# Mixture-of-experts stage: another order of the experts' steps, a 32-slot form for the smallest expert, seven weight tiles

## The chip, the cores and the metric

The kernel runs on one core of one Trainium2 chip, as one program. The metric is the device time in microseconds (us) of one execution. Lower is better.

## The reference, cut to what matters

Two transformer blocks run one after the other on 256 tokens of width 1024, in fp32. The change lies in the mixture of experts (MoE) at the end of the first block:

```
def _moe(h, router, w1, w3, w2):
    ...
    top_v, top_i = lax.top_k(logits, TOP_K)            # 2 of 8 experts per token
    top_w = jax.nn.softmax(top_v, axis=-1)
    gates = ...                                        # [256, 8], two entries per token
    for e in range(N_EXPERTS):
        y = y + gates[:, e:e + 1] * _swiglu(hf, w1[e], w3[e], w2[e])
```

`_swiglu` is silu(x w1) * (x w3), times w2, with w1 and w3 of 1024 x 3584 and w2 of 3584 x 1024. One expert's weights are 44 MB in fp32, eight are 352 MB. Which expert a token goes to is known only at run time.

## The kernel before, in words

Each expert's tokens are gathered into a fixed number of slots by a product with a 0/1 matrix, pass through the expert, and are scattered back by a second product (`scatter`), which adds gate * result to `k.y`. After the routing the experts are ranked by how many tokens they got. Expert "0" is always expert number FIRST, and 1 to 7 follow by falling count. Below, E0 to E7 are these ranks. `base_of` (line 220) gives the slots: 160 for E1, 64 for E5, E6 and E7 (`SMALL`), 128 for the others. If an expert got more tokens than slots, a branch after the stage (line 1351) handles the rest.

An expert's weights come as 42 units of 1 MB (28 of w1 and w3, 14 of w2). `k.unit` (line 239) takes the next of a ring of `MOE_RING` = 6 raw tiles and issues its DMA on SP's queue, in program order. A tile is free again when the work that reads it is done.

There are three ways of multiplying:

- **128 slots** (`expert`). `k.split` (lines 254, 255) splits half a unit into a high part `wh` (copied on ScalarE, "ACT") and a low part `wl` (subtracted on VectorE, "DVE"). Both come from the pool `k.whl`, with four buffers each. `mm3` (lines 266 to 268) makes three fp32r products of 512 columns on TensorE ("PE") out of each of the four 512-column pieces of a unit: 12 products a unit.
- **64 slots** (`small_expert`). Plain fp32 products straight from the raw tile, with the token block as the stationary operand of 64 columns, in two column groups of the array (lines 1192 and 1206). No split is needed.
- **E1's slots 128 to 159** (`extra`). The same in four column groups of 32 (lines 1090 and 1114), inside E1's loop. The raw tile is thus read by the split and by these products. The trace shows each plain fp32 product as two matmul instructions.

`expert` and `small_expert` are generators. One step of an expert (`run(todo[r], 1)`) is a block of 512 hidden units: four units of w1 and w3, silu and multiplication, then two units of w2 for the block before, then the transposition of the new hidden block. An expert has seven steps and an end (`run(todo[r])`) with the last two units of w2. The first step has no w2, so it has four units. `late` holds a finished expert's scatter until another expert calls `settle()`.

Order before: four steps of E0; preparation of E1; a step of E0; preparation of E5 to E7 (`smalls`); the rest of E0; then seven pairs of steps E1, E5; seven pairs E2, E6; E3 alone; E4 with E7, where E7 begins two steps later. E7 therefore has two steps and its end left when E4 is through. In between `y` is multiplied by a gate row and added to `Xx` (lines 1323 and 1324), and E4's and E7's scatters: E7 adds straight to `Xx` (mode "last"). Then the final norms are computed and the branch is taken.

The program is put in order by a scheduler at build time. It keeps each engine's instructions roughly, but not strictly, in the order in which the source issues them.

PSUM in this stage: `pA` has three banks (products, transpositions), `pO` two, `pX` three (the accumulators `po`). E0 accumulates in `pO`, E1 to E4 in `pX`, E5 to E7 in `pO`.

Of the kernel before, what the change touches and what calls it, by code (L numbers as in the profile page):

```python
# [213 lines left out]
MOE_RING = 6  # L214
CAP1 = 160
SMALL = (5, 6, 7)
LAST = 7


def base_of(r):  # L220

    return CAP1 if r == 1 else 64 if r in SMALL else 128

# [682 lines left out]
def moe(k):  # L906
# [147 lines left out]

    def expert(r, e, xe, ST, mode="add", extra=None):
# [12 lines left out]
        pool, name = (k.pO, "psO") if r == 0 else (k.pX, "psX")  # L1068
        po = [pool.tile([128, 512], F32, name=name) for _ in range(2 if extra is None else 3)]
        hid = None  # L1070
        for b in range(8):
            if b < 7:
                pss = []
                if extra is not None:
                    px = k.pA.tile([128, 512], F32, name="psA")
                for z in range(2):
                    ps = k.pA.tile([128, 512], F32, name="psA")
                    for h in range(2):
                        raw = k.unit(src(b * 4 + z * 2 + h))
                        for q in range(2):  # L1080
                            w = k.split(raw[:, q * 1024:(q + 1) * 1024], 1024)
                            for kk in range(2):
                                kc = h * 4 + q * 2 + kk
                                sl = slice(kk * 512, (kk + 1) * 512)
                                k.mm3(ps, (xH[:, kc, :], xL[:, kc, :]), (w[0][:, sl], w[1][:, sl]), kc == 0, kc == 7)
                        if extra is not None:
                            for kc in range(4 * h, 4 * h + 4):
                                for j in range(4):
                                    o = (kc % 4) * 512 + j * 128
                                    nc.tensor.matmul(px[32 * j:32 * j + 32, z * 128:(z + 1) * 128], xex[:, kc, :],  # L1090
                                                     raw[:, o:o + 128], start=(kc == 0), stop=(kc == 7))
                    pss.append(ps)
                s = k.tmp.tile([128, 512], F32, name="act", bufs=k.nact)
                nc.scalar.activation(s, pss[0], AF.Silu)
                m = k.tmp.tile([128, 512], F32, name="act2", tag="act", bufs=k.nact)
                nc.vector.tensor_mul(m, s, pss[1])
                if extra is not None:
                    sx = k.tmp.tile([128, 512], F32, name="actx", tag="act", bufs=k.nact)
                    nc.scalar.activation(sx[:, :128], px[:, 0:128], AF.Silu)
                    nc.vector.tensor_mul(sx[:, 128:256], sx[:, :128], px[:, 128:256])  # L1100
            settle()
            if b > 0:
                for u in (2 * b - 2, 2 * b - 1):
                    raw = k.unit(src(28 + u))
                    for q in range(2):
                        c = u * 2 + q
                        w = k.split(raw[:, q * 1024:(q + 1) * 1024], 1024)
                        cs = slice((c % 4) * 128, (c % 4) * 128 + 128)
                        for d in range(2):
                            sl = slice(d * 512, (d + 1) * 512)  # L1110
                            k.mm3(po[d], (hid[0][:, cs], hid[1][:, cs]), (w[0][:, sl], w[1][:, sl]), c == 0, c == 27)
                        if extra is not None:
                            for j in range(4):
                                nc.tensor.matmul(po[2][32 * j:32 * j + 32, 0:256], hid[2][:, 32 * (c % 4):32 * (c % 4) + 32],
                                                 raw[:, q * 1024 + j * 256:q * 1024 + (j + 1) * 256],
                                                 start=(c == 0), stop=(c == 27))
            if b < 7:
                pt = k.pA.tile([128, 512], F32, name="psA")
                for q in range(4):
                    nc.tensor.transpose(pt[:, q * 128:(q + 1) * 128], m[:, q * 128:(q + 1) * 128], k.ident)  # L1120
                hH = p.tile([128, 512], F32R, name=tag + "H", bufs=2)
                hL = p.tile([128, 512], F32R, name=tag + "L", bufs=2)
                nc.scalar.copy(hH, pt)
                nc.vector.tensor_sub(hL, pt, hH.bitcast(F32))
                hid = [hH, hL]
                if extra is not None:
                    pt = k.pA.tile([128, 512], F32, name="psA")
                    nc.tensor.transpose(pt[:, :128], sx[:, 128:256], k.ident)
                    hx = p.tile([128, 128], F32, name="hxx", bufs=2)
                    nc.vector.tensor_copy(hx, pt[:, :128])  # L1130
                    hid.append(hx)
                yield True
# [11 lines left out]
        if extra is not None:  # L1144
            oxs = []
            for d in range(2):
                ox = k.tmp.tile([128, 512], F32, name="ox", tag="act", bufs=k.nact)
                nc.gpsimd.memset(ox, 0.0)
                for j in range(2 * d, 2 * d + 2):
                    js = slice(32 * j, 32 * j + 32)  # L1150
                    nc.scalar.copy(ox[js, (j % 2) * 256:(j % 2) * 256 + 256], po[2][js, 0:256])
                oxs.append(ox)
# [20 lines left out]
    def small_expert(r, e, xf, i, Sd, mode="add"):  # L1173
# [41 lines left out]
        o = po  # L1215
        if mode == "last":
            o = k.tmp.tile([128, 512], F32, name="og", tag="act", bufs=k.nact)
            for t in range(2):
                ts_ = slice(64 * t, 64 * t + 64)
                nc.vector.tensor_mul(o[ts_, :], po[ts_, :], k.gate5[ts_, t * 512:(t + 1) * 512])  # L1220
        oH = p.tile([128, 512], F32R, name="oH", tag="hidH", bufs=2)
        oL = p.tile([128, 512], F32R, name="oL", tag="hidL", bufs=2)
        nc.scalar.copy(oH, o)
        nc.vector.tensor_sub(oL, o, oH.bitcast(F32))

        def scatter():
            for d in range(2):
                for t in range(2):
# [6 lines left out]
                    y = k.Xx if mode == "last" else k.y  # L1235
                    nc.vector.scalar_tensor_tensor(y[:, t, sl], ps, g, y[:, t, sl], op0=ALU.mult, op1=ALU.add)
# [17 lines left out]
    def smalls():  # L1254
# [5 lines left out]
        xf = gather(S, 64 * len(SMALL), "xs")  # L1260
        out = []
        for i in range(len(SMALL)):
# [7 lines left out]
            Z = p.tile([128, 512], F32R, name="Sz", tag="Sz" if SMALL[i] == LAST else "hxH",  # L1270
                       bufs=1 if SMALL[i] == LAST else 2)
# [5 lines left out]
        return out  # L1277
# [10 lines left out]
    Sx = p.tile([128, 2, 4, 32], F32R, name="Sx")  # L1288
    for t in range(2):
        nc.vector.tensor_copy(Sx[:, t], S[:, t, 128:160].bitcast(F32).unsqueeze(1).to_broadcast([128, 4, 32]))  # L1290
    SxT = slots_T(Sx.rearrange("p t j s -> p t (j s)"), "SxT")
    STx = slots_T(S[:, :, 0:128], "ST1")
    todo = {1: expert(1, index(1), xe, STx, "add", (xex, SxT.bitcast(F32)))}
    run(g, 1)
    for r, made in zip(SMALL, smalls()):
        todo[r] = small_expert(r, index(r), *made, "last" if r == LAST else "add")
    run(g)
    pairs = {}

    def start(r):  # L1300
        if r in (2, 3, 4):
            if r not in pairs:
                pairs.update(zip((r, r + 1), pair(r)))
            xf, z, ST = pairs[r]
            todo[r] = expert(r, index(r), parts(xf, z), ST)

    for one, other in ((1, 5), (2, 6), (3, None), (4, 7)):
        start(one)
        for b in range(7):
            run(todo[one], 1)  # L1310
            if other is not None and (other != LAST or b > 1):
                run(todo[other], 1)
        if one == 3:
# [3 lines left out]
        run(todo[one])  # L1317
        if other not in (None, LAST):
            run(todo[other])
    over = nc.values_load(infoi[0:1, 16:17], engines=ALL_ENGINES, min_val=0, max_val=256)  # L1320
    run(todo[LAST], 1)
    for t in range(2):
        nc.vector.tensor_mul(k.y[:, t, :], k.y[:, t, :], k.gate5)
        nc.vector.tensor_add(k.Xx[:, t, :], k.Xx[:, t, :], k.y[:, t, :])
    run(todo[LAST], 1)
    g = todo[LAST]
# [24 lines left out]
    with k.tc.If(over > 0):  # L1351
        for r in (0, 1, 2, 3) + SMALL:
# [553 lines left out]
def build(nc, tc, a, o):  # L1906
    with ExitStack() as es0:
# [6 lines left out]
        k.whl = k.pool("whl", 4)  # L1914
# [14 lines left out]
        with ExitStack() as es1:  # L1929
            k.es = es1  # L1930
            k.pA = k.pool("pA", 4, space=PSUM)
# [19 lines left out]
        with ExitStack() as es1:  # L1951
# [6 lines left out]
            k.pX = k.pool("pX2", 3, space=PSUM)  # L1958
            extra = k.pool("wraw2", MOE_RING - 5)
# [3 lines left out]
        with ExitStack() as es1:  # L1963
            k.es = es1
            k.nxn, k.nact = 2, 5
            k.tmp = k.pool("tmp4", 2)
            k.h2 = k.pool("h2")
# [23 lines left out]
```

## Time and profile before

| what | value |
|---|---|
| median of 3 runs | 2272.66 us (2270.87 to 2274.89) |
| the profiled execution | 2272.78 us |
| its span, first to last instruction | 2269.8 us |
| outside the span | 3.0 us |
| TensorE's mean granted clock | 0.983 of 2.4 GHz |
| PE / DVE / ACT busy | 2167.8 / 1413.6 / 1007.1 us |
| read from HBM | 546.08 MB |

The profiled execution is 0.1 us above the median, so it stands for it. The MoE's products run from about 797 to 1785 us of the span. PE's busy time counts overlapping instructions once, so inside the stage the starts of instructions say more than their durations.

### The profile page before, as it was taken

What the parts mean: (1) busy time and instruction counts of PE and PEld (TensorE: products, weight loads), DVE (VectorE), ACT (ScalarE), POOL (GpSimd) and SP (SyncE); (2) the same over time, 40 slices, a digit from 0 to 9 for tenths busy, and PEclk for the clock granted to TensorE, in tenths of its full rate; (3) what the DMA queues carried; (4) which work ended last, traced back from release to release, by engine and by line L of the source; (5) the groups of instructions that cost most, each with busy time, mean ns of one, the idle gap of its engine ahead of it and who ended that gap; (6) DMA issues with size and microseconds to landing.
All of it is one profiled execution on the core that took longest, in us unless ns stands there. A gap on an engine that the chain in (4) does not pass through costs nothing. (4 is left out here: it accounts for less than half of the span.)

```text
span 2269.8 us, 31775 instructions
## 1 busy us (share of the span) xinstructions
PE 2167.8 (96%) x12353; PEld 1639.3 (72%) x12353; DVE 1413.6 (62%) x2391; ACT 1007.1 (44%) x1452; POOL 51.0 (2%) x101
## 2 busy tenths in 40 slices
PE   6999999999999899999999999999999699999998
PEld 3777778788786777766656666677765477798997
DVE  4899339534555687743436454888555487866555
ACT  4234322222345477543335444677443344454443
POOL 1000000000000000000000000000000000000000
PEclk7999999999999999999999999999999899999999
DMA  9553545431543286788888999898999643344552
GB/s 369 213 201 120 210 149 195 162 140 49 170 170 112 99 310 263 289 338 342 330 347 316 413 421 421 342 361 312 348 421 421 267 154 117 107 165 166 186 186 75
DMA packets 82112, 554.55 MB, mean 244 GB/s; under 512 B 9905, under 2 KB 10161, under 8 KB 19233
## 3 DMA queue, kind: packets, MB, share of 16 engines
q1 hardware_dynamic: 75600, 531.87, 61.3%
q0 software_dynamic: 6208, 19.52, 2.5%
q8 instruction: 99, 1.62, 0.3%
q10 hardware_dynamic: 144, 1.05, 0.1%
q14 instruction: 61, 0.49, 0.1%
HBM read 546.08 MB, written 6.32 MB: 243 GB/s over the span
## 5 line engine op out<-in xcount | busy, mean ns | idle before, releaser
L255 DVE TENSOR_TENSOR wl<-raw,wh 128x1024 fp32r<-128x1024 f32 x664 | 791.5, 1215 | 379.3 <-ACT wh L254 372.8
L254 ACT CAST wh<-raw 128x1024 fp32r<-128x1024 f32 x664 | 679.3, 1045 | 651.6 <-PE psA L267 176.0
L266 PE MATMUL psA<-wh,xeH 128*128 128x512 f32 x560 | 228.3, 408 | 2.7 <-ACT wh L254 1.2
L267 PE MATMUL psA<-wl,xeH 128*128 128x512 f32 x560 | 226.3, 404 | 4.4 <-DVE wl L255 4.4
L268 PE MATMUL psA<-wh,xeL 128*128 128x512 f32 x560 | 223.1, 398 | 0.1
L266 PE MATMUL psG<-hH,wh 128*128 128x256 f32 x544 | 157.8, 290 | 1.0 <-DVE hL L699 1.0
L266 PE MATMUL psA<-xTH,wh 128*128 128x512 f32 x400 | 157.3, 393 | 0.0
L268 PE MATMUL psG<-hH,wl 128*128 128x256 f32 x544 | 155.8, 286 | 0.0
L267 PE MATMUL psA<-xTL,wh 128*128 128x512 f32 x400 | 155.7, 389 | 0.0
L268 PE MATMUL psA<-xTH,wl 128*128 128x512 f32 x400 | 155.7, 389 | 0.0
L267 PE MATMUL psG<-hL,wh 128*128 128x256 f32 x544 | 155.1, 285 | 0.0
L1192 PE MATMUL psA<-raw,xs 128*64 128x256 f32 x1344 | 150.3, 381 | 0.8 <-DMA raw<-in_moe_dram 0.4
L266 PEld LDWEIGHTS psA<-wh,xeH 128*128 128x128 f32 x560 | 106.3, 190 | 41.1 <-ACT wh L254 11.3
L1192 PEld LDWEIGHTS psA<-raw,xs 128*64 128x64 f32 x1344 | 94.5, 137 | 53.0 <-issue 5.3
L267 PEld LDWEIGHTS psA<-wl,xeH 128*128 128x128 f32 x560 | 106.5, 190 | 35.9 <-DVE wl L255 12.2
L268 PEld LDWEIGHTS psA<-wh,xeL 128*128 128x128 f32 x560 | 106.3, 190 | 25.0 <-DVE xeL L1046 0.9
L266 PEld LDWEIGHTS psG<-hH,wh 128*128 128x128 f32 x544 | 103.9, 191 | 13.3 <-issue 11.2
L268 PEld LDWEIGHTS psG<-hH,wl 128*128 128x128 f32 x544 | 103.9, 191 | 6.3 <-issue 6.2
L267 PEld LDWEIGHTS psG<-hL,wh 128*128 128x128 f32 x544 | 104.0, 191 | 3.3 <-issue 2.7
L1196 DVE TENSOR_TENSOR act<-act,psA 128x256 f32<-128x256 f32 x21 | 8.8, 421 | 141.2 <-ACT act L1195 141.2
L266 PEld LDWEIGHTS psA<-xTH,wh 128*128 128x128 f32 x400 | 75.1, 188 | 25.4 <-ACT wh L254 8.4
L267 PE MATMUL psX<-wl,hidH 128*128 128x512 f32 x224 | 89.9, 401 | 0.0
(576 smaller groups left out, 3776.8 us busy)
## 6 DMA issues: line engine op xcount, KB each, us to landing
raw<-in_moe_dram SPq DMA_DIRECT2D x336, 1024.0 KB, 7.4
raw<-in_w_ada_dram SPq DMA_DIRECT2D x48, 1024.0 KB, 6.4
raw<-in_w2ff_dram SPq DMA_DIRECT2D x32, 1024.0 KB, 4.8
raw<-in_w2mix_dram SPq DMA_DIRECT2D x24, 1024.0 KB, 4.8
raw<-in_eff_dram SPq DMA_DIRECT2D x22, 1024.0 KB, 4.9
raw<-in_eff_dram SPq DMA_DIRECT2D x22, 512.0 KB, 3.3
raw<-in_ein_dram SPq DMA_DIRECT2D x8, 1024.0 KB, 7.0
raw<-in_w2in_dram SPq DMA_DIRECT2D x8, 1024.0 KB, 9.3
```

The costliest lines, as they stand in the source:

```text
L254: self.nc.scalar.copy(h[:, :n], src)
L255: self.nc.vector.tensor_sub(l[:, :n], src, h[:, :n].bitcast(F32))
L266: mm(ps, s[0], m[0], start=first, stop=False)
L267: mm(ps, s[0], m[1], start=False, stop=False)
L268: mm(ps, s[1], m[0], start=False, stop=last)
L1192: nc.tensor.matmul(px[64 * t:64 * t + 64, z * 256:(z + 1) * 256], xf[:, kc, xs], raw[:, o:o + 256], start=(kc == 0), stop=(kc == 7))
L1196: nc.vector.tensor_mul(m[:, 256:512], m[:, 0:256], px[:, 256:512])
```

## The change

It gives the experts' steps another order, written out by hand (`ORDER`: a number is one step, a negative number -n the end of expert n-1). E7 gets 32 slots and its own generator, `tiny_expert`, which uses products like those of `extra`. These products are grouped: for E1, both halves of w1 or w3 behind each other after the 24 fp32r products (before: after each half), and a whole unit of w2 at once. The ring has seven raw tiles; for that `k.whl` has three buffers in this stage in place of four. E0 accumulates in `pX`. E4's scatter now goes to `Xx` too. E1's and the small experts' preparations come one behind the other, after four steps of E0. `gate5` and the load of `over` are issued at E3's first step, the fold of `y` into `Xx` after E4's first step.

```diff
-MOE_RING = 6
+MOE_RING = 7
-SMALL = (5, 6, 7)
-LAST = 7
+ORDER = ([0, 5, 0, 5, 0, 5, -1] + [1, 6, 5] * 4 + [-6] + [1, 6, 7, 1, 6, 7, 1, 6, -2, -7]
+         + [2, 2, 2, 2, 7, 2, 2, 2, -3] + [3, 7, 3, 3, 3, 3, 7, 3, 3, -4] + [4, 4, 7, 4, 4, 4, 4, 7, 4, -5])
+SMALL = (5, 6)
+TINY = 7
...
+    return CAP1 if r == 1 else 64 if r in SMALL else 32 if r == TINY else 128
...
+    def tiny_in(px, x, raw, z, h):
+        for kc in range(4 * h, 4 * h + 4):
+            for j in range(4):
+                o = (kc % 4) * 512 + j * 128
+                nc.tensor.matmul(px[32 * j:32 * j + 32, z * 128:(z + 1) * 128], x[:, kc, :],
+                                 raw[:, o:o + 128], start=(kc == 0), stop=(kc == 7))
...
+    def tiny_out(po, hx, raw, u):
+        for q in range(2):
+            c = u * 2 + q
+            for j in range(4):
+                nc.tensor.matmul(po[32 * j:32 * j + 32, 0:256], hx[:, 32 * (c % 4):32 * (c % 4) + 32],
+                                 raw[:, q * 1024 + j * 256:q * 1024 + (j + 1) * 256], start=(c == 0), stop=(c == 27))
...
+    def tiny_expert(r, e, x, SxT):
...
+        for b in range(8):
+            if b < 7:
+                px = k.pA.tile([128, 512], F32, name="psA")
+                for z in range(2):
+                    for h in range(2):
+                        tiny_in(px, x, k.unit(src(b * 4 + z * 2 + h)), z, h)
+                sx = tiny_gate(px)
+                settle()
+            if b > 0:
+                for u in (2 * b - 2, 2 * b - 1):
+                    tiny_out(po, hx, k.unit(src(28 + u)), u)
+            if b < 7:
+                hx = tiny_hid(sx)
+                yield True
...
+                    nc.tensor.matmul(ps, SxT[:, t * 128:(t + 1) * 128], oxs[d], start=True, stop=True)
...
-        pool, name = (k.pO, "psO") if r == 0 else (k.pX, "psX")
-        po = [pool.tile([128, 512], F32, name=name) for _ in range(2 if extra is None else 3)]
+        po = [k.pX.tile([128, 512], F32, name="psX") for _ in range(2 if extra is None else 3)]
...
-                        if extra is not None:
-                            for kc in range(4 * h, 4 * h + 4):
...
+                    if extra is not None:
+                        for h in range(2):
+                            tiny_in(px, xex, raws[h], z, h)
...
+                    if extra is not None:
+                        tiny_out(po[2], hid[2], raw, u)
...
-    run(g, 1)
-    for r, made in zip(SMALL, smalls()):
-        todo[r] = small_expert(r, index(r), *made, "last" if r == LAST else "add")
-    run(g)
+    made, (x7, S7) = smalls()
...
+    for r in ORDER:
+        if r < 0:
+            run(todo[-r - 1])
+            continue
+        if r not in todo:
+            start(r)
+        run(todo[r], 1)
...
-        k.whl = k.pool("whl", 4)
...
+            k.whl = k.pool("whl2", 3)
```

## Rows read from the trace of the kernel before

**Rows 1.** The page: engines' busy time; DMA issues (KB each, us to landing).
```profile
PE 2167.8 (96%) x12353; PEld 1639.3 (72%) x12353; DVE 1413.6 (62%) x2391; ACT 1007.1 (44%) x1452; POOL 51.0 (2%) x101
...
raw<-in_moe_dram SPq DMA_DIRECT2D x336, 1024.0 KB, 7.4
```

**Rows 2.** Windows: us; busy per engine (instructions); PE clock, DMA share, GB/s.
```profile
797.00:945.00 148.00, 141.36 (x679) 113.04 (x682) 123.44 (x145) 112.67 (x135) 0.00 (x0) 0.99 0.76 290
945.00:1200.00 255.00, 253.73 (x2179) 159.09 (x2172) 110.99 (x119) 94.91 (x119) 1.05 (x2) 1.00 0.87 335
1260.00:1400.00 140.00, 135.12 (x720) 92.38 (x718) 77.97 (x74) 68.07 (x78) 0.00 (x0) 1.00 1.01 421
1440.00:1600.00 160.00, 156.36 (x694) 123.20 (x693) 138.05 (x133) 117.03 (x134) 0.00 (x0) 1.00 0.88 334
1660.00:1760.00 100.00, 97.14 (x562) 63.58 (x563) 51.89 (x53) 37.77 (x47) 0.00 (x0) 1.00 1.01 420
```

**Rows 3.** Timeline of PE: 128-slot experts' transpositions, E0 alone, then E4 with E7.
```profile
845.02 0.60 PE L1120 MATMUL psA<-identt,act 128*128 128x128 f32 x4
...
862.25 0.60 PE L1120 MATMUL psA<-identt,act 128*128 128x128 f32 x4
...
1693.57 0.60 PE L1120 MATMUL psA<-identt,act 128*128 128x128 f32 x4
...
1723.14 0.60 PE L1120 MATMUL psA<-identt,act 128*128 128x128 f32 x4
```

**Rows 4.** Timeline of PE: one step of a 64-slot expert (start us, us).
```profile
1369.74 7.13 PE L1192 MATMUL psA<-raw,xs 128*64 128x256 f32 x64
1377.81 0.44 PE L1210 MATMUL psA<-identt,act 128*128 128x128 f32 x2 [0.94 <-DVE act L1196]
1378.18 3.65 PE L1206 MATMUL psO<-raw,hids 128*64 128x512 f32 x16
```

**Rows 5.** Groups by line, 783 to 1810 us: busy us, mean ns, idle before.
```profile
L1090 PEld LDWEIGHTS psA<-raw,xex 128*32 128x32 f32 x896 | 23.8, 109 | 12.1 <-issue 11.5 <-ACT wh L254 0.4 <-PE psA L1210 0.2
...
L1162 PE MATMUL psA<-ox,SxT 128*128 128x512 f32 x8 | 4.1, 591 | 0.0
...
L1323 DVE TENSOR_TENSOR y<-y,gate 128x1024 f32<-128x1024 f32 x2 | 2.3, 1214 | 0.0
```

**Rows 6.** Timeline of PE: blocks of 32-slot products inside E1's steps.
```profile
1154.67 0.62 PE L1090 MATMUL psA<-raw,xex 128*32 128x128 f32 x10
...
1161.43 0.39 PE L268 MATMUL psA<-wh,xeL 128*128 128x512 f32 x1
1161.75 1.08 PE L1090 MATMUL psA<-raw,xex 128*32 128x128 f32 x32
1162.77 0.50 PE L266 MATMUL psA<-wh,xeH 128*128 128x512 f32 x1
1163.10 0.40 PE L267 MATMUL psA<-wl,xeH 128*128 128x512 f32 x1
...
1187.12 1.07 PE L1114 MATMUL psX<-raw,hxx 128*32 128x256 f32 x16
```

**Rows 7.** Timeline of PE: the stage's last waits.
```profile
1774.62 5.25 PE L1206 MATMUL psO<-raw,hids 128*64 128x512 f32 x16 [3.12 <-DMA raw<-in_moe_dram]
1782.06 0.97 PE L1232 MATMUL psA<-oH,Sz 128*128 128x512 f32 x3 [2.19 <-ACT oH L1223]
```

**Rows 8.** Timeline of DVE, ACT and PE: one pair `wh`, `wl` in E0.
```profile
836.54 2.60 DVE L255 TENSOR_TENSOR wl<-raw,wh 128x1024 fp32r<-128x1024 f32 x2 [0.21 <-ACT wh L254]
...
836.82 1.06 ACT L254 CAST wh<-raw 128x1024 fp32r<-128x1024 f32 x1 [0.32 <-PE psA L268]
...
838.22 1.06 ACT L254 CAST wh<-raw 128x1024 fp32r<-128x1024 f32 x1 [0.34 <-PE psA L268]
...
840.46 0.68 DVE L1096 TENSOR_TENSOR act<-act,psA 128x512 f32<-128x512 f32 x1
...
841.05 0.40 PE L267 MATMUL psO<-wl,hidH 128*128 128x512 f32 x1
```

More of the change, by code (lines that the diff above doesn't have):

```diff
@@ new lines, in tiny_rows @@
+    def tiny_rows(po, gate=False):
+        oxs = []
+        for d in range(2):
+            ox = k.tmp.tile([128, 512], F32, name="ox", tag="act", bufs=k.nact)
+            nc.gpsimd.memset(ox, 0.0)
+            for j in range(2 * d, 2 * d + 2):
+                js = slice(32 * j, 32 * j + 32)
+                to = ox[js, (j % 2) * 256:(j % 2) * 256 + 256]
+                if gate:
+                    nc.vector.tensor_mul(to, po[js, 0:256], k.gate5[js, j * 256:(j + 1) * 256])
+                else:
+                    nc.scalar.copy(to, po[js, 0:256])
+            oxs.append(ox)
+        return oxs
@@ L1144, in expert @@
         if extra is not None:
[L1145 to L1152, printed above, removed]
+            oxs = tiny_rows(po[2])
         def scatter():
@@ L1214, in small_expert @@
         settle()
[L1215 to L1220, printed above, removed]
         oH = p.tile([128, 512], F32R, name="oH", tag="hidH", bufs=2)
         oL = p.tile([128, 512], F32R, name="oL", tag="hidL", bufs=2)
-        nc.scalar.copy(oH, o)
-        nc.vector.tensor_sub(oL, o, oH.bitcast(F32))
+        nc.scalar.copy(oH, po)
+        nc.vector.tensor_sub(oL, po, oH.bitcast(F32))
         def scatter():
@@ L1276, in smalls, with spread @@
             out.append((xf, i, Z))
-        return out
+        return out, (xf[:, :, 128:160], spread(S, 128, "SxT7"))
+    def spread(S, base, name):
+        Sx = p.tile([128, 2, 4, 32], F32R, name="Sx")
+        for t in range(2):
+            nc.vector.tensor_copy(Sx[:, t], S[:, t, base:base + 32].bitcast(F32).unsqueeze(1).to_broadcast([128, 4, 32]))
+        return slots_T(Sx.rearrange("p t j s -> p t (j s)"), name)
     xe = parts(gather(S0), 0)
@@ L1287, in moe @@
     nc.vector.tensor_copy(xex, xf[:, :, 128:160])
[L1288 to L1291, printed above, removed]
+    SxT = spread(S, 128, "SxT")
     STx = slots_T(S[:, :, 0:128], "ST1")
     todo = {1: expert(1, index(1), xe, STx, "add", (xex, SxT.bitcast(F32)))}
-    run(g, 1)
-    for r, made in zip(SMALL, smalls()):
-        todo[r] = small_expert(r, index(r), *made, "last" if r == LAST else "add")
-    run(g)
+    made, (x7, S7) = smalls()
+    for r, m in zip(SMALL, made):
+        todo[r] = small_expert(r, index(r), *m)
+    todo[TINY] = tiny_expert(TINY, index(TINY), x7, S7.bitcast(F32))
+    todo[0] = g
     pairs = {}
@@ L1304, in start @@
             xf, z, ST = pairs[r]
[L1305 to L1313, printed above, removed]
+            todo[r] = expert(r, index(r), parts(xf, z), ST, "last" if r == 4 else "add")
+    for r in ORDER:
[5 more added lines that the diff above has]
+        run(todo[r], 1)
+        if r == 3 and "fold" not in pairs:
+            pairs["fold"] = True
             k.gate5 = gate_rows(k, 1, 5, 0)
@@ L1316, in moe @@
             nc.gpsimd.dma_start(k.fg, a["rowf"][0:1, :].to_broadcast([128, 1024]))
[L1317 to L1326, printed above, removed]
+            over = nc.values_load(infoi[0:1, 16:17], engines=ALL_ENGINES, min_val=0, max_val=256)
+        if r == 4 and "y" not in pairs:
+            pairs["y"] = True
+            for t in range(2):
+                nc.vector.tensor_mul(k.y[:, t, :], k.y[:, t, :], k.gate5)
+                nc.vector.tensor_add(k.Xx[:, t, :], k.Xx[:, t, :], k.y[:, t, :])
+    g = todo[TINY]
     raw = k.unit(a["w2in"][0])
@@ L1351, in moe @@
     with k.tc.If(over > 0):
-        for r in (0, 1, 2, 3) + SMALL:
+        for r in (0, 1, 2, 3) + SMALL + (TINY,):
             base = base_of(r)
```

60 lines of the change are left out of this document (36 added, 24 removed).

## The prediction

> **What bounds the kernel now.** I read the page first: PE is busy for 2167.8 of 2269.8 us, and the MoE's weights come as 336 transfers of 1 MB [rows 1]. Busy PE time overlaps itself, so it only says where to look. The windows by stage come next [rows 2]. Where E0 runs alone (797 to 945) and E3 alone (1440 to 1600), PE has work nearly all the time and DMA stands at 0.76 and 0.88. With E1 and E5 together it is 0.87. With E2 and E6, and with E4 and E7, DMA is full: 1.01 share, 421 GB/s, one unit in 1.049 MB / 421 = 2.49 us. PE idles there for under 4% (135.12 of 140, 97.14 of 100). So PE is the bound, and in two stages DMA runs level with it. All 336 units need 837 us at that rate, and the stage lasts from 797 to 1785, 988 us. There is room for less PE work if the transfers spread evenly.
>
> The timeline gives PE's price of each form of step. E0 alone goes from transposition to transposition in 17.23 us, 2.87 a unit; E4 with E7 in 29.57 [rows 3]. E7's 64-slot step thus costs 29.57 - 17.23 = 12.34. The rows of such a step agree: 7.13 of products, 0.94 of waiting for the evicted hidden block, two transpositions, 3.65 of w2 [rows 4]; the next piece of PE work starts 12.0 after the first. It reads six units, which take DMA 14.9. A big step reads six in 17.23 and is PE's. So PE time per byte, not the number of tokens, is what mixing has to balance.
>
> **The sum**, against the profiled execution's 2272.8 us (0.1 above the median, so the two are the same here).
>
> *E7 on 32 slots.* Its step has 128 matmul instructions for w1 and w3 and 32 for w2. In E1 such products run in four column groups at once, and a group of four is paced by its weight load, 0.109 us [rows 5]: 32 groups make 3.5 us. Sixteen w2 products take 1.07 [rows 6], so 32 in one block take about 1.8. Entering and leaving such a block costs something: from the big product before to the big one behind are 1.34 us, and the next spacing is 0.33 [rows 6]. The normal spacing is 0.23 (72 products in 17.23 us, less the transpositions). So the block costs 1.34 + 0.33 - 2 x 0.23 = 1.21, of which 8 x 0.109 = 0.87 is streaming and 0.34 the switch. Two blocks, one transposition (0.3) and the same 0.94 wait give 3.5 + 1.8 + 0.7 + 0.3 + 0.9 = 7.2 us. That saves 5.1 us a step, **36 us** in seven. Without the wait it would be 42. At the pace of the worst block, ten in 0.62 us [rows 6], the 160 products would take 9.9, and with transposition and wait 11.1, so only 8 would be saved.
>
> *E1's products grouped.* The PE timeline of E1 shows 36 blocks for w1 and w3 (20 of 32 instructions, eight halves cut in two) and 28 for w2. The new source asks for 14 and 14, 36 fewer: 12 us at 0.34. The order is made by a scheduler that has cut eight of 28 blocks already, so I allow for eight cuts again and take **10** (0 to 12).
>
> *E6 and E5 beside other work.* E6 goes from E2, where DMA was full, to E1. If other work fills its 0.94 us wait, seven steps gain 6.6. I take **3** (0 to 6.6).
>
> *The tail.* Before, E7 has two steps and its end left when E4 is through. PE then waits 3.12 us for a transfer and 2.19 for a cast [rows 7]. After, only E7's last two units and two scatters are left; they are in the ring by then. The transfer's wait and one eviction wait go: **4** (0 to 6). Something like the cast stays.
>
> *What is added.*
> - E7's scatter is plain fp32: eight instructions of this kind take 4.1 us together in E1 [rows 5], against 8 x 0.23 for the fp32r products: **+2** (0 to 2.3).
> - The fold of `y` moves from the tail, where DVE had time, into E4's steps. Its four operations of 1.21 us [rows 5] make 4.9 us. The low parts stand ready 1.9 us before use at best: **+3** (0 to 4.9).
> - The two preparations come one behind the other. PE idled 6.6 us in the window that holds them [rows 2]; I add **+2** (0 to 4) because no step of E0 lies between them.
> - The third split pair. A pair's low part was ready at 839.14 and first used at 841.05, 1.91 us later [rows 8]. ACT starts a copy when PE lets a pair go, every 1.40 us. With three pairs the copy starts 1.40 later, so 0.5 us of lead is left. The loop closes: 1.06 of copy, 1.30 of subtraction and 1.40 of products are 3.8 in the 4.2 that three pairs give. A DVE job of 0.68 [rows 8] can push through 0.5 of lead by 0.2. There are two such jobs in each of 35 big steps: 14 us if all hit. Most come behind the transpositions or after a small step, which refill the pairs: **+3** (0 to 14).
> - The seventh raw tile covers the tiny steps. A tiny step takes six units in 7.2 us, while DMA brings 2.9; four big steps of 17.23 bring back 4 x 0.9. That closes. In the rounds E1, E6, E7 two light steps follow each other, take twelve units in about 19 us and get 7.6, while E1's step gains 3 to 4. Twice in a row this falls short by a unit: **+2** (0 to 6).
>
> The cover for the loads of `over` and the gate row is POOL's and SP's own idle time; they stay at nothing, unless SP waits there with transfers behind it, which the +2 holds. SP issues the same 336 transfers. Expert overflow isn't taken up by this sum: on these inputs the reference's router gives the two smallest experts 11 and 16 tokens, so 32 slots do.
>
> -36 - 10 - 3 - 4 + 2 + 3 + 2 + 3 + 2 = -41, so **2232 us**. With all ends at their best: -42 - 12 - 6.6 - 6 = -67 (2206). With all at their worst: -8 + 31 = +23 (2296).
>
> **A rule against it.** The trace shows 32 of the narrow products in 1.08 us, 34 ns each, and ten in 0.62, 62 ns each [rows 6]. The Trainium skill, page "TensorE: Matmul & The Clock Gate", section "Wait — 56ns, not 53.3ns?", says that with hardware decode off the sequencer spends about 62 ns on each MATMUL, which becomes the bound when the array's work is shorter. By it E7's step would take 11 us and the sum would be about -13. The block of 32 speaks against it, by that section's own condition.
>
> **Rivals.**
> 1. *The narrow products are paced one by one.* At 62 ns each, as in the block of ten, E7 saves 8 in place of 36: 2260. For it: that block. Against: 20 blocks of 32 at half the price. 7%.
> 2. *The blocks don't merge*, because the scheduler issues them whenever a split is late. Without the 10: 2242. For it: it cut eight halves before. 14%.
> 3. *The tiny steps wait for DMA.* If two of six units are late in each of seven steps, 7 x 2 x 2.49 = 35 us go: 2267. For it: the full DMA of two stages [rows 2]. Against: the ring holds seven, a step needs six. 9%.
> 4. *The third pair turns the split into the bound*, and it gets slower. The place is E2 to E4, where DVE has 12 x 1.30 + 2 x 0.68 = 17.0 us of work in 17.23. If each of 70 DVE jobs costs its whole 0.68 the loss is 48 us. If ACT's job ahead of each does as much again, it is 95. Midway, 72 in place of 3: 2301. It decides from 44 us on, 0.105 us in each of 420 half units. Against: three pairs' loop of 3.8 in 4.2. 6%.
> 5. *More waits go than I count*: DMA no longer level with PE, no eviction wait in E7, merged blocks, no late split: 2215. 12%.
> 6. *It doesn't do what it says*: the scheduler puts the steps back to much the old mix, and time comes out within a few us of before. 2%.
>
> **How the numbers follow.** My forecast has 50%. A measurement of this kernel can tell about 0.2% from no change, 4.5 us. Forecast, rivals 1, 2 and 5 and most of 3 are faster by more; part of 3 and 6 lie within; 4 is slower. Faster 0.89, same 0.05, slower 0.06. The range reaches from 2210 (forecast with E7's wait gone, full merging and the tail at its best; rival 5) to 2258 (forecast with the added terms near their ends, rival 2, nearly rival 1). Rivals 3, 4 and 6 and a little below 2210 stay outside.
>
> **What the changed profile would show.** Right: the last MoE scatter near 1744 us instead of 1785; E7's step at about 7 us on PE with blocks of 128 and 32; 28 to 36 blocks in E1; DMA near 0.95 in all stages and nowhere flat at 1.01 for 100 us; PE waits on `wl` of a few us in all. Wrong: PE waiting for `raw` from DMA in E7's products (rival 3); waits on `wh` and `wl` of tens of us (rival 4); E7's products at more than 40 ns each (rival 1); blocks in E1 as many as before (rival 2); a gap behind E1's preparation of more than 5 us.

## The result, and the profile after

The changed kernel takes **2244.62 us** (median of 4 runs, 2243.41 to 2248.14); the kernel before, beside it on the same chip, 2271.76. The ratio is 0.9884, with a 95% interval of 0.9864 to 0.9903: 27 us faster. Forecast were 41 (2232), in a range of 2210 to 2258. The profiled execution took 2245.74 us, its span is 2244.0.

All of it lies in the MoE stage. Counted from the first split product to the last scatter, the stage ran from 797.3 to 1784.9 before and runs from 797.6 to 1760.1 after; what follows it takes 485 us before and 484 after. One row of windows says it all, here of the kernel before and then of the changed one (us; busy time of each engine with instructions; granted PE clock, DMA share, GB/s):

```profile
797.30:1784.90 987.60, 953.98 (x5727) 664.32 (x5727) 596.97 (x621) 510.90 (x614) 1.05 (x2) 0.99 0.90 354
```

```profile
797.60:1760.10 962.50, 917.67 (x6282) 663.12 (x6280) 606.25 (x631) 518.08 (x606) 2.10 (x4) 0.99 0.91 365
```

PE's busy time falls by 36 us, as much as E7's term of the forecast. But the stage gets only 25 shorter: PE's idle time in it rises from 33.6 (987.6 - 953.98) to 44.8 us. What PE waited for shows the rest. First the waits of PE in that stretch before, then after (who waits, for whom: us in total, times, longest):

```profile
PE psA L1210 <- DVE act L1196: 12.2, 13, 0.9
PE psA L267 <- DVE wl L255: 4.4, 5, 2.2
PE psO L1206 <- DMA raw<-in_moe_dram: 3.1, 1, 3.1
PE psA L1232 <- ACT oH L1223: 2.2, 1, 2.2
...
PE psA L266 <- ACT wh L254: 1.2, 2, 0.9
```

```profile
PE psA L269 <- ACT wh L257: 12.4, 9, 2.2
PE psA L270 <- DVE wl L258: 7.4, 8, 2.3
PE psA L1275 <- DVE act L1261: 6.6, 7, 0.9
PE psA L1074 <- DVE actx L1069: 4.3, 6, 0.7
...
PE psA L1132 <- DVE ox L1096: 2.1, 1, 2.1
...
PE psO L1083 <- DMA raw<-in_moe_dram: 1.4, 1, 1.4
...
PE psA L1224 <- ACT oH L1213: 1.0, 1, 1.0
```

The waits on evicted hidden blocks (12.2 before, 6.6 + 4.3 after) and those of the tail (3.1 + 2.2 [rows 7], now 2.1 + 1.0) shrink a little. The new ones are on `wh` (1.2 to 12.4) and `wl` (4.4 to 7.4).

The windows by stage, after: E0 alone and with E5; E1 with E6, E5 and E7; E2; E3; E4. They answer to [rows 2].

```profile
797.00:945.00 148.00, 140.65 (x692) 107.97 (x693) 104.17 (x129) 97.20 (x121) 0.00 (x0) 0.97 0.79 308
988.00:1288.00 300.00, 282.81 (x2564) 180.33 (x2556) 109.14 (x120) 91.31 (x114) 1.05 (x2) 0.98 0.93 375
1337.00:1468.00 131.00, 129.79 (x703) 102.79 (x701) 110.98 (x105) 92.63 (x98) 0.00 (x0) 1.00 0.96 383
1468.00:1616.00 148.00, 141.35 (x899) 111.13 (x898) 116.62 (x113) 104.08 (x117) 0.00 (x0) 1.00 0.95 385
1616.00:1744.00 128.00, 121.01 (x790) 94.68 (x791) 100.58 (x96) 81.91 (x87) 1.05 (x2) 0.99 0.93 374
```

The transfers are spread as foreseen: 0.93 to 0.96 from 988 on, and no longer 1.01 for 100 us as with E2, E6 and E4, E7 before. Where E1 runs, PE was idle for 0.5% of the time before (253.73 of 255 busy [rows 2]) and is idle for 6% now (282.81 of 300 busy).

E7's step on PE's timeline (start us, us; in brackets the idle time before it), the counterpart of [rows 4]:

```profile
1389.84 3.70 PE L1063 MATMUL psA<-raw,xs 128*32 128x128 f32 x128
1394.26 0.33 PE L1074 MATMUL psA<-identt,actx 128*128 128x128 f32 x1 [0.72 <-DVE actx L1069]
1394.52 1.93 PE L1083 MATMUL psO<-raw,hxx 128*32 128x256 f32 x32
1396.38 0.51 PE L269 MATMUL psA<-wh,xeH 128*128 128x512 f32 x1
```

From 1389.84 to 1396.38 are 6.54 us; 7.2 were forecast. The 64-slot step before took 12.0 counted in the same way, and 12.34 in the sum. The 128 products take 3.70 us, 29 ns each, in one block.

To see what each kind of work gave, I took the time from each PE instruction's start to the next one's, less the idle time, over the stage, and summed it by kind:

| us | before | after | difference | forecast |
|---|---|---|---|---|
| E7, out of the 64-slot products | 77.5 | 40.2 | -37.3 | -36 |
| E1's narrow products | 47.2 | 47.9 | +0.7 | -10 |
| fp32r products | 614.3 | 612.1 | -2.2 | 0 |
| preparations and scatters | 42.0 | 45.0 | +3.0 | +2 |
| idle | 33.2 | 44.4 | +11.2 | +3 |

77.5 is what the 64-slot products took less, 226.5 to 149.0; the transpositions (-0.4) are left out. The forecast's idle time is the -3, -4, +3, +2, +3 and +2 of the sum (the +2 for the preparations was argued from PE's idle time there). A block of narrow products costs time in two rows: in its own, and in that of the fp32r products, which start 0.33 us apart beside a block and 0.23 elsewhere ([rows 6]). So the grouping's -10 faces +0.7 and -2.2 together. Two terms fail: the grouping gives little, and idle time rises. The experiments are about these two, and about which of the change's parts the 27 us hang on.

### The profile page after: what moved, and what is told of

Same layout as the page of the kernel before. It is cut to its first block, busy times and chain, and to the rows that moved or that the text cites. A ratio compares the mean times of both kernels' runs of the same rounds, so it can differ in the third digit from the quotient of the medians.

```text
span 2244.0 us, 32899 instructions
## 1 busy us (share of the span) xinstructions
PE 2130.6 (95%) x12906; PEld 1638.2 (73%) x12906; DVE 1420.7 (63%) x2401; ACT 1014.4 (45%) x1443; POOL 51.6 (2%) x102
## 3 DMA queue, kind: packets, MB, share of 16 engines
q8 instruction: 103, 1.69, 0.3%
## 5 line engine op out<-in xcount | busy, mean ns | idle before, releaser
L257 ACT CAST wh<-raw 128x1024 fp32r<-128x1024 f32 x664 | 690.3, 1047 | 703.2 <-PE psA L271 188.5
L269 PE MATMUL psA<-wh,xeH 128*128 128x512 f32 x560 | 227.0, 405 | 13.7 <-ACT wh L257 12.4
L270 PEld LDWEIGHTS psA<-wl,xeH 128*128 128x128 f32 x560 | 106.8, 191 | 42.8 <-DVE wl L258 16.3
L269 PEld LDWEIGHTS psG<-hH,wh 128*128 128x128 f32 x544 | 103.9, 191 | 13.3 <-issue 11.2
L270 PE MATMUL psX<-wl,hidH 128*128 128x512 f32 x280 | 111.9, 399 | 0.0
L271 PE MATMUL psX<-wh,hidL 128*128 128x512 f32 x280 | 110.7, 395 | 0.0
L269 PE MATMUL psX<-wh,hidH 128*128 128x512 f32 x280 | 101.8, 400 | 0.0
L1257 PE MATMUL psA<-raw,xs 128*64 128x256 f32 x896 | 99.6, 380 | 0.3 <-DVE y L1230 0.3
```

The source lines that it names most:

```text
L257: self.nc.scalar.copy(h[:, :n], src)
L269: mm(ps, s[0], m[0], start=first, stop=False)
L270: mm(ps, s[0], m[1], start=False, stop=False)
L271: mm(ps, s[1], m[0], start=False, stop=last)
L1257: nc.tensor.matmul(px[64 * t:64 * t + 64, z * 256:(z + 1) * 256], xf[:, kc, xs], raw[:, o:o + 256], start=(kc == 0), stop=(kc == 7))
```

## The experiments

Every kernel is the changed one with the edit shown, unless it says otherwise. The kernel before, run beside them, had medians of 2271.8, 2271.3 (e5 to e8), 2270.0 (e9 to e11) and 2272.4 us (e12). The traced runs of e2, e3, e6 and e11 were 5 to 6 us faster than their medians.

### The parts of the change

**e1_ungrouped**: E1's w1 and w3 products behind each half again.

```diff
-                    if extra is not None:
-                        for h in range(2):
-                            tiny_in(px, xex, raws[h], z, h)
+                        if extra is not None:
+                            tiny_in(px, xex, raw, z, h)
```

> The changed kernel, but E1's narrow products of w1 and w3 stand behind each half again, as before. Changed kernel: 2244.6 us. Theory: grouping brought little, because the scheduler cut the grouped products again (34 blocks, 36 before), and it makes E1 hold two raw tiles until the narrow products are done, which starves the ring. Then ungrouping gives 2 to 8 us back (2237 to 2243), and PE's waits for wh (12.4 us in the stage) fall below 8. Rival: grouping is worth the 10 us that the prediction gave it, or the 4 us by which the narrow blocks and the spacing around them fell: then it is slower, 2248 to 2255.

Measured: 2244.0 us, ratio 0.9879 [0.9856, 0.9902]. That is no difference that these runs can tell (the interval is 5 us wide to either side), and it lies between the two ranges, so neither the theory nor its rival is borne out. The two traces show why: two effects stand against each other. In the changed kernel the scheduler cuts the 128 narrow products of a step into blocks of 26, 16, 22, 2 and 62 in six of seven steps, 34 blocks in all, where there were 36; in e1 it makes 42. With the fp32r spacings beside them, e1's blocks take 3.8 us more. But PE idles 2 us less in e1's stage (42.8 against 44.8), and its waits on `wh` are 10.2 us in place of 12.4. E1's w2 products are grouped in both, so this run says nothing of them.

**e2_ring6_pairs4**: ring and pairs as before the change.

```diff
-MOE_RING = 7
+MOE_RING = 6
...
-            k.whl = k.pool("whl2", 3)
+            k.whl = k.pool("whl2", 4)
```

> The changed kernel with six raw tiles and four split pairs, the sizes before. Theory: the third pair costs nothing (E3's steps last 17.35 us in both kernels), the seventh raw tile saves DMA waits where two light steps follow each other: slower, 2248 to 2256, with PE's waits for wh and raw above 18 us in all (13.8 in the changed kernel). Rival: the missing fourth pair is what makes PE wait for wh and wl (19.8 us together): then 2234 to 2240 and these waits fall below 10 us.

Measured: 2267.2 us, ratio 0.9982 [0.9966, 0.9998]. Neither range holds it: nearly the whole gain is gone without the seventh tile, far more than I had expected. The trade that the change makes, a pair for a tile, is thus worth 23 us.

**e3_old_order**: the order of before (E1 with E5, E2 with E6, E3, E4 with E7).

```diff
+ORDER = ([0, 0, 0, -1] + [1, 5] * 7 + [-2, -6] + [2, 6] * 7 + [-3, -7] + [3] * 7 + [-4]
+         + [4, 4] + [4, 7] * 5 + [-5, 7, 7])
```

> The changed kernel with the steps in the old order (E1 with E5, E2 with E6, E3 alone, E4 with E7, two of E7's steps at the end), all else as changed: 32 slots, grouping, seven tiles. Theory: most of the gain is the 32 slots (about 40 us of PE work), and the even mix is worth only what the tail and E6's wait brought, less its own DMA waits: 2243 to 2252. Rival: without the mix the light steps meet a full DMA in E4 with E7 and the gain is mostly lost: above 2256. Other rival: the new order's DMA waits cost more than its tail saves: 2230 to 2241.

Measured: 2265.84 us, ratio 0.9975 [0.9959, 0.999]. The rival holds: without the even mix 32 slots, grouping and ring together bring 6 us. The windows of e3 show E4 with E7 at the end:

```profile
1620.00:1760.00 140.00, 117.33 (x1256) 86.05 (x1254) 65.00 (x71) 49.82 (x59) 1.05 (x2) 0.89 1.01 420
```

The transfers are full for 140 us, PE idles for 23 of them, and what it does it does at a clock of 0.89. Near its end the products of three units in a row (32 instructions each) stand behind a transfer:

```profile
1744.93 1.08 PE L1063 MATMUL psA<-raw,xs 128*32 128x128 f32 x32 [0.98 <-DMA raw<-in_moe_dram]
1747.42 1.08 PE L1063 MATMUL psA<-raw,xs 128*32 128x128 f32 x32 [1.41 <-DMA raw<-in_moe_dram]
1749.89 1.08 PE L1063 MATMUL psA<-raw,xs 128*32 128x128 f32 x32 [1.39 <-DMA raw<-in_moe_dram]
```

One unit in 2.49 us: the rate of a full DMA, which the prediction took from [rows 2].

**e7_64_slots**: order, ring and grouping of the change, but E7 as a third 64-slot expert, with the code of the kernel before.

```diff
-    return CAP1 if r == 1 else 64 if r in SMALL else 32 if r == TINY else 128
+    return CAP1 if r == 1 else 64 if r in SMALL or r == TINY else 128
...
+    for r, m in zip(SMALL + (TINY,), smalls()):
+        todo[r] = small_expert(r, index(r), *m, "last" if r == TINY else "add")
...
```

> The changed kernel with its order, seven tiles and grouping, but E7 on 64 slots as the kernel before had it; so what the 32 slots are worth once the order is even. Theory (with an even order nearly all of PE's saving of 37 us reaches the end, where in the old order only some 6 did): 2268 to 2280 us, PE idle 35 to 44 us. Rival (the transfers set the end in either order, so that 32 slots bring a third of it or less): 2250 to 2258 us, PE idle under 25 us.

Measured: 2272.84 us, ratio 1.0007 [0.9992, 1.0023]. The theory holds. With the new order 32 slots are worth 28 us; order and ring without them are worth nothing that these runs can tell. e7's stage:

```profile
798.40:1785.90 987.50, 947.56 (x5729) 669.91 (x5727) 604.90 (x623) 520.77 (x615) 1.05 (x2) 0.99 0.90 356
```

PE is busy for 30 us more than after, and idle for 39.9.

**e5_ring6**: six tiles, three pairs.

```diff
-MOE_RING = 7
+MOE_RING = 6
```

> The changed kernel with six raw tiles in place of seven, its three split pairs kept; so it differs from e2 by the pair alone. Theory (the tile is what paid, the pair is worth nothing): 2264 to 2270 us, within 3 us of e2's 2267, PE idle in the MoE stage 53 to 60 us, of it some 7 on raw tiles. Rival (e2 lost its time because of the fourth pair, or the tile matters only where four pairs run ahead): 2243 to 2255 us.

Measured: 2273.57 us, ratio 1.001 [0.9995, 1.0026]: the gain is gone without the seventh tile. The tile is worth 29 us with three pairs; e2's fourth pair gave 6 of them back, where I had expected no more than 3. PE's waits and the stage, e5:

```profile
PE psA L269 <- ACT wh L257: 20.9, 12, 2.7
...
PE psA L1063 <- DMA raw<-in_moe_dram: 4.3, 4, 1.4
PE psO L1083 <- DMA raw<-in_moe_dram: 2.9, 3, 2.0
```

```profile
793.60:1784.00 990.40, 930.94 (x6280) 669.88 (x6280) 605.51 (x623) 519.10 (x609) 2.10 (x4) 0.97 0.90 356
```

The stage is 27.9 us longer than after. 14.6 are idle time (990.40 - 930.94 against 44.8). The other 13.3 are PE's busy time for the same instructions, at a granted clock of 0.97 in place of 0.99. So over this stage the added waits are paid nearly twice.

So the change's parts don't add. Against the kernel before, the change without its order is worth -6 us, without the 32 slots +1.5, without the tile +2.3 (neither of these two is clear of noise), and with all three -27.

### Where the added idle time comes from

**e4_fold_spread**: the four operations of the fold one by one after E4's first four steps.

```diff
-        if r == 4 and "y" not in pairs:
-            pairs["y"] = True
-            for t in range(2):
+        if r == 4 and pairs.setdefault("y", 0) < 4:
+            t = pairs["y"] // 2
+            if pairs["y"] % 2 == 0:
                 nc.vector.tensor_mul(k.y[:, t, :], k.y[:, t, :], k.gate5)
+            else:
                 nc.vector.tensor_add(k.Xx[:, t, :], k.Xx[:, t, :], k.y[:, t, :])
+            pairs["y"] += 1
```

> The changed kernel, but the four DVE operations that fold y into Xx are issued one after each of E4's first four steps instead of all after its first. Theory: they hold back the low parts in E4's second step, which lasts 22.2 us instead of 17.3: 4 to 5 us come back (2239 to 2241), and that step falls below 18.5. Rival: the step is long because of the preparation of E4 and its scatter, not the fold: within 1.5 us of the changed kernel.

Measured: 2238.9 us, ratio 0.986 [0.9835, 0.9885], 6 us under the changed kernel. The theory holds (to 0.1 us of its range). On DVE's timeline of the changed kernel the four operations of the fold stand ahead of the low parts `wl`:

```profile
1618.41 2.35 DVE L1386 TENSOR_TENSOR y<-y,gate 128x1024 f32<-128x1024 f32 x2
1620.68 2.35 DVE L1387 TENSOR_TENSOR Xx<-Xx,y 128x1024 f32<-128x1024 f32 x2
1622.95 3.49 DVE L258 TENSOR_TENSOR wl<-raw,wh 128x1024 fp32r<-128x1024 f32 x3
```

And PE waits, in E4's second step:

```profile
1621.41 0.49 PE L269 MATMUL psA<-wh,xeH 128*128 128x512 f32 x1 [0.90 <-ACT wh L257]
1624.22 0.50 PE L270 MATMUL psA<-wl,xeH 128*128 128x512 f32 x1 [2.32 <-DVE wl L258]
...
1626.17 0.63 PE L270 MATMUL psA<-wl,xeH 128*128 128x512 f32 x1
1626.60 0.63 PE L271 MATMUL psA<-wh,xeL 128*128 128x512 f32 x1
...
1629.36 0.40 PE L271 MATMUL psA<-wh,xeL 128*128 128x512 f32 x1
1629.60 0.39 PE L269 MATMUL psA<-wh,xeH 128*128 128x512 f32 x1
```

The 72 products of this step take 22.16 us (1617.24 to 1639.40), those of E4's later steps 17.00. Of the 5.2 more, 3.22 are waits; most of the rest comes because behind them seven products follow each other every 0.43 us in place of 0.235. The granted clock of that stretch (a window from 1621 to 1629) was at 1.2 GHz, the lower of its two levels, for part of the time:

```profile
1621.00:1629.00 8.00, 5.27 (x15) 3.97 (x16) 6.66 (x6) 1.86 (x3) 0.00 (x0) 0.79 0.33 108
```

In e4 the waits on `wl` fall from 7.4 to 4.1 us, and from E4's first transposition to its third are 39.17 us in place of 43.69. So 4.5 of the 6 us lie there; where the rest lies isn't shown, and it is within the noise.

**e6_one_light**: e4 with an order in which no two light steps follow each other; E7 ends early, so its gate rows are loaded at E1's first step, and E4's end comes last.

```diff
+ORDER = ([0, 5, 0, 5, 0, 5, -1] + [1, 7] * 7 + [-2, -8] + [2, 5] * 4 + [-6] + [2, 6] * 3 + [-3]
+         + [3, 6] * 4 + [-7] + [3, 3, 3, -4] + [4] * 7)
...
+        if r == 1 and "rows" not in pairs:
+            pairs["rows"] = True
+            k.gate5 = gate_rows(k, 1, 5, 0)
...
-    g = todo[TINY]
+    g = todo[4]
```

> All parts of the change kept and the fold spread as in e4, but another order: never two light steps behind each other; E5 beside E0 and E2, E7's seven 32-slot steps beside E1's seven, E6 beside E2 and E3, E4 alone at the end. Theory (PE's waits on wh and raw come where two light steps want 12 units in some 24 us, which the ring can't hold): the 1.4 us wait ahead of each of E1's first products goes, PE idle in the stage 25 to 33 us in place of 42 to 44, 2226 to 2236 us. Rival (the transfers are full over the whole stretch, so a wait taken from one place comes back at another): idle 38 to 44 us, 2236 to 2243 us like e4. Against both, if 32-slot steps beside E1 starve (12 units in 30.5 us against about 29.6 at the fastest rate seen): over 2243 us.

Measured: 2243.23 us, ratio 0.9884 [0.9864, 0.9903]; PE idle in the stage 40.8 us. The theory fell, and the rival holds, with the time at the end of its range: the waits of 1.42 us ahead of E1's steps went, but others came, on transfers in E1's rounds with E7 and on evictions of 64-slot blocks (11.3 us in place of 6.6).

**e8_one_light_ring6**: e6 with `MOE_RING = 6`.

> e6 with six raw tiles. Theory (the seventh tile pays by carrying bursts of two light steps; with one at a time little is left to carry): at most 8 us over e6, 2230 to 2242 us, PE idle under 40 us. Rival (the tile is lead time everywhere, whatever the order): 14 to 22 us over e6, 2244 to 2258 us, PE idle 40 to 55 us.

Measured: 2267.06 us, ratio 0.9982 [0.9966, 0.9998], 24 over e6, more than even the rival had. The tile is no cover for pairs of light steps alone; it is lead in every order tried.

**e9_ring8_pairs2**: the trade once more, a pair for a tile.

```diff
-MOE_RING = 7
+MOE_RING = 8
...
-            k.whl = k.pool("whl2", 3)
+            k.whl = k.pool("whl2", 2)
```

> The changed kernel with the trade taken one step further: eight raw tiles and two split pairs. Theory (in E0 to E4 the split of one half unit takes 1.9 us from start to end and its products 1.4 us, so with two pairs a pair comes back every 3.3 us for two half units, 1.65 us each against 1.40): some 0.2 us on each of the 280 half units of steps that stand alone, 2275 to 2340 us, PE idle on wl above 40 us. Rival (lead in raw tiles is all that counts): 2225 to 2240 us.

Measured: 2372.08 us, ratio 1.0461 [1.0441, 1.048], slower still than the theory's end. PE's waits in e9, up to 1800 us of the span:

```profile
PE psA L270 <- DVE wl L258: 55.6, 137, 3.1
```

and two transpositions in E3 on its timeline:

```profile
1462.82 0.60 PE L1196 MATMUL psA<-identt,act 128*128 128x128 f32 x4
1485.33 0.60 PE L1196 MATMUL psA<-identt,act 128*128 128x128 f32 x4
```

A step of E3 takes 22.51 us, 1.876 a half unit; with three pairs it takes 17.36 (1506.22 to 1523.58 after), with the four of before 17.35 (1491.81 to 1509.16). The prediction's loop for a pair was 1.06 of copy, 1.30 of subtraction and 1.40 of products, 3.76; shared by two pairs that is 1.88 a half unit. The loop was right. The expectation had 1.9 for copy and subtraction, which are 2.36.

**e10_ring8_pairs3**: e4 with eight tiles and three pairs. The room comes from one set of token tiles.

```diff
-MOE_RING = 7
+MOE_RING = 8
...
-            H, L = [p.tile([128, 8, 128], F32R, name="xe" + part, bufs=2) for part in "HL"]
+            H, L = [p.tile([128, 8, 128], F32R, name="xe" + part, bufs=1) for part in "HL"]
...
-    xe = parts(xf, 0)
+    xf1 = xf
...
+        if r == 1:
+            todo[1] = expert(1, index(1), parts(xf1, 0), STx, "add", (xex, SxT.bitcast(F32)))
...
```

> e4 (fold spread) with eight raw tiles and three split pairs; the room comes from one set of token tiles for the experts in place of two, for which E1's set is made when E0 has ended. Theory (the ring's lead is what is short: six to seven tiles took 14.7 us of PE's waits and some 10 us of lower clock away): the waits on wh and raw, 11.6 us in e4, halve, PE idle 30 to 35 us, 2224 to 2236 us. Rival (seven are enough, the eighth buys nothing; E1's later set costs 1 to 2 us): 2236 to 2243 us.

Measured: **2227.83 us**, ratio 0.9812 [0.9796, 0.9828], 11 under e4. The waits on transfers in E1's and E3's steps go but for one, those on `wl` fall to 1.4 us. Three waits of 1.42 us on `wh` stay, each ahead of a step of E1, to the hundredth as after, although there is a tile more:

```profile
1009.05 0.51 PE L269 MATMUL psA<-wh,xeH 128*128 128x512 f32 x1 [1.42 <-ACT wh L257]
1058.84 0.49 PE L269 MATMUL psA<-wh,xeH 128*128 128x512 f32 x1 [1.42 <-ACT wh L257]
1108.62 0.49 PE L269 MATMUL psA<-wh,xeH 128*128 128x512 f32 x1 [1.42 <-ACT wh L257]
```

So these are not the transfers' doing. ACT's timeline shows what stands ahead of that `wh` (the changed kernel):

```profile
1057.29 0.38 ACT L1260 ACTIVATE act<-psA 128x256 f32<-128x256 f32 x1 [6.53 <-PE psA L1257]
1062.25 0.37 ACT L1277 COPY hids<-psA 128x256 f32<-128x256 f32 x1 [4.58 <-PE psO L1271]
1062.52 2.00 ACT L257 CAST wh<-raw 128x1024 fp32r<-128x1024 f32 x2
```

The copy of E5's hidden block has its input at 1058.6 but waits for the w2 products of the same step to end (L1271), because `hids` has two tiles and two 64-slot experts now take turns with them: the tile it gets is the one which these products still read. Before, one 64-slot expert ran at a time, and in e6, where E5 and E6 take no turns, these waits were gone too.

**e11_ring8_old_order**: e10 with e3's order.

> e10 with the order of e3 (E7 beside E4 at the end). Theory (lead can't replace the mix: five rounds of E4 and E7 want 60 units in some 120 us, where the fastest rate seen brings one in 2.5 us, so 28 us are missing and one more tile carries 2.5 of them): 2250 to 2262 us, the transfers at 1.01 from 1620 to 1760 us. Rival (an eighth tile makes the order indifferent): 2228 to 2240 us.

Measured: 2255.29 us, ratio 0.9939 [0.9925, 0.9954], 27 over e10. The theory holds; from 1620 to 1760 the transfers are at 1.01 again. Lead doesn't replace the mix.

**e12_hids3**: e10 with three `hids` tiles.

```diff
-                hid = p.tile([128, 256], F32, name="hids", bufs=2)
+                hid = p.tile([128, 256], F32, name="hids", bufs=3)
```

> e10 with three tiles in place of two for the 64-slot experts' transposed hidden block (hids), which E5 and E6 share. Theory (in a round of E1, E6, E5 the copy of E5's block must wait till E5's w2 products have let its own last tile go, 4.58 us, and on ACT the first wh of E1's next step stands behind it; so it is neither the ring nor the transfers): the three waits of 1.42 us ahead of E1's steps go, the one of 1.63 us behind E6's end stays, PE waits on wh 4 to 5 us in place of 8.6, 2221 to 2226 us. Rival (E1's first unit is late anyway, with the transfers at 1.01 there, so the wait is the same and only its releaser changes): wh stays at 8 to 9 us, 2226 to 2231 us.

Measured: **2221.79 us**, ratio 0.9783 [0.9764, 0.9803]. The theory holds: waits on `wh` are 4.5 us, and the copy now waits 0.99 us, for its own transposition, with `wh` close behind it while PE does the w2 products (ACT's timeline, e12):

```profile
1053.19 0.37 ACT L1277 COPY hids<-psA 128x256 f32<-128x256 f32 x1 [0.99 <-PE psA L1275]
1053.46 2.94 ACT L257 CAST wh<-raw 128x1024 fp32r<-128x1024 f32 x3
```

Its stage, for comparison with the two at the top:

```profile
796.90:1735.90 939.00, 909.88 (x6280) 659.03 (x6280) 604.21 (x627) 515.95 (x606) 2.10 (x4) 0.99 0.93 373
```

939.0 us, 29.1 of them idle. It is the fastest kernel of this study, 51 us under the kernel before.

## Why the prediction was right, and where not

The sign, the bound and the largest term were right. Point by point:

- **E7 on 32 slots, -36: right.** Its products, wait and step measured 3.70, 0.72 and 6.54 us against 3.5, 0.94 and 7.2; PE's own time fell by 37.3. What the sum didn't say is that this term holds only beside the order (e3: 6 us of it reach the end) and the ring (e5: none). I had priced the order only by small terms of its own. But E7 in old order makes the stretch with E4 a DMA stretch, and PE's saving there is answered by waits.
- **Pacing by single products (rival 1): fell.** The trace has 29 ns a product in a block of 128. The 62 ns that the Trainium skill, page "TensorE: Matmul & The Clock Gate", section "Wait — 56ns, not 53.3ns?", gives for each MATMUL with hardware decode off would have made 7.9 us of these 3.70, by estimate; no run here shows such a floor.
- **E1's products grouped, -10: wrong.** The step that failed is "I allow for eight cuts again": the new source asks for 36 blocks fewer, with eight cuts it would have been 28, and 15 went. The scheduler cut the w1 and w3 products into 34 blocks, two fewer than before (the outcome of rival 2; why the scheduler cuts where it does isn't shown). Only the w2 products merged, 28 blocks to 15. The price held: with the fp32r spacings on both sides the w2 blocks cost 4.1 us less, 0.32 for each that went, against 0.34. But two blocks of 26 took 1.7 us more than the others of that size, at a lower clock (last section), so that little was left.
- **E5 and E6 beside other work, -3: nothing, and a new wait beside it.** The eviction waits of E5 and E6 stayed at 6.6 us, seven of 0.94 (before, 6.6 of the 12.2 lay between 890 and 1440). And E5 and E6 side by side share two `hids` tiles, and the copy that waits for a tile holds up E1's first `wh` on ACT. That is three waits of 1.42 in the changed kernel; e12 took them away, and 6 us went. The prediction asked what is queued behind a waiting instruction on DVE and SP, and not here on ACT.
- **The tail, -4:** mis-sized. 5.3 us of waits became 3.1, with a new one of 2.08 on E7's gated rows.
- **The fold of `y`, +3: mis-sized.** e4 shows 4.5 in the two steps that it touches, and 6 in the median: 3.22 are waiting in one step, and behind it comes a slower clock.
- **E7's scatter and the preparations, +2 each:** 3.0 together, as PE's own time. For the preparations +2 was meant as idle time: PE's waits on `xf`, `xs`, `Sd` and `Sx` are 4.4 us over the stage before and 4.2 after.
- **The third pair, +3 (rival 4): nothing where an expert runs alone.** E3's step takes 17.36 us, as before. e9 shows the loop of 3.76 at work with two pairs, so three hold with the margin that the prediction gave. In the mixed stretches it isn't shown to be nothing: beside six tiles the fourth pair is worth 6 us (e2 against e5).
- **The ring, +2: mis-sized.** Three late `wh` behind E7 steps in E1 and E3 (1.24, 1.69 and 2.21, with ACT waiting for DMA) and one late `raw` (1.41) make 6.5 us of idle time, with a slower clock behind those in E1 and none behind the 2.21 in E3. I had counted units that were missing twice in a row. That a tile is worth 29 us, as e5 shows, stood nowhere: I had taken the seventh tile for the cover of the tiny steps alone; e8 shows that it is needed in another order as much, and e10 that an eighth goes on giving, 11 us.

The grouping missed by 8.5 (over both of its rows) and the idle time by 8.2; the other rows came out 0.7 better. So -41 became -25 in the stage, and -27 in the median. The range held it because it took in rival 2 and the ends of the added terms. That the time lies close to rival 2's 2242 is in part luck: that rival had only one half of the miss, and idle time isn't in it.

Seven tiles with all four pairs were not tried. A pair takes as much room as a tile, so with e10's one set of token tiles they would fit, and what the fourth pair would give there is open. The 13 us of added busy time in e5 are for the most part the clock's: its trace has TensorE at the lower level for 54.6 us of the stage, that of the changed kernel for 27.3, and PE works in 48.8 and 24.3 of them. At 0.43 us a product in place of 0.235 this makes about 11 us, an estimate from these numbers.

## What to carry to other kernels

Price parts of a change together where they share a resource: here any two of fewer PE instructions, an even mix and a longer ring gave 6 us at best, all three 27. Where a pair of split buffers and a raw tile cost the same room, the tile carries twice the data; count the loop of the pairs (copy, subtraction, products over their number) and give the rest to the ring. When two generators that ran one after the other are interleaved, look at every tile name they share, and at what stands behind the waiting writer on its engine.

## What the runs showed of the hardware

- A PE wait can cost more than its length. Behind the 0.90 and 2.32 us in E4's second step, products came every 0.43 us instead of 0.235, and the granted clock was 0.79 from 1621 to 1629; over e5's whole stage the same instructions took 13.3 us more of busy time, at a granted clock of 0.97. The Trainium skill, page "TensorE: Matmul & The Clock Gate", section "HAM oscillation — how this bites in real kernels", describes this of waits of some 3 to 5 us for a transfer: behind each, the next products begin at the lower clock. The rows here agree, for shorter waits, and a wait on VectorE did it (the 2.32) as well as those on a transfer (1.41 and 1.69 in E1; the granted clock was 0.50 from 1257 to 1264). But not every wait does it: behind 1.42 us ahead of a step of E1 the clock stayed at 1.00 (1063 to 1066), and behind 2.21 in E3 too (1549 to 1560). What decides between them isn't shown.
- A block of 26 narrow products took 1.06 us behind one wait of 1.42, and 1.89 where two waits lay ahead of it, 0.72 and 1.24; the granted clock was 1.00 from 1063 to 1066 and 0.77 from 1210 to 1214 (PE's timeline of the changed kernel):

```profile
1063.62 0.49 PE L269 MATMUL psA<-wh,xeH 128*128 128x512 f32 x1 [1.42 <-ACT wh L257]
1064.04 1.06 PE L1063 MATMUL psA<-raw,xex 128*32 128x128 f32 x26
...
1210.09 0.33 PE L1074 MATMUL psA<-identt,actx 128*128 128x128 f32 x1 [0.72 <-DVE actx L1069]
1211.66 0.50 PE L269 MATMUL psA<-wh,xeH 128*128 128x512 f32 x1 [1.24 <-ACT wh L257]
1212.09 1.89 PE L1063 MATMUL psA<-raw,xex 128*32 128x128 f32 x26
```

- Where a wait is named by `wh` on ACT, its cause was a transfer in some cases and a tile of another expert in others; only ACT's own timeline, or a run with more of the one resource, tells them apart.
